# Low weight parts of the channel projection formed by ScalarE and an accumulating DMA; the second norm's token scale applied behind the down projection

## The chip, the cores and the metric

The kernel runs on one core of a Trainium2 chip. The metric is the device time of one execution in microseconds, the median over runs. The core's engines, by the names of the profile, are PE (TensorE, the matmuls), DVE (VectorE), ACT (ScalarE), POOL (GpSimd) and SP (SyncE, which issues nearly all DMAs). Each engine works through its own list of instructions in a fixed order and waits at an instruction until what it needs is there; 16 DMA engines move data beside them.

## The reference, cut to what matters

One layer of a hybrid decoder, on 512 prompt tokens and 8 x 8 sample tokens (576 in all), with a model width of 1024:

```python
x = residual
xn = rmsnorm(x, g1)
u = xn @ W_in                       # channels (q, k, v, gate) of the gated-delta mixer,
                                    # and q, k, v of the window attention
o = concat(gated_delta(conv(u)), dilated_attention(u))
h = x + o @ W_out
z = rmsnorm(h, g2)                  # h * g2 * R, one scale R for each token
y = h + (relu(z @ W_up) ** 2) @ W_down      # W_up 1024 x 4096, W_down 4096 x 1024
```

As relu(R a)^2 = R^2 relu(a)^2 for a positive R, the token scale R of the second norm can stand in front of the up projection, behind its relu, or behind the down projection as R^2.

## The kernel before, in words

**Products.** Every float32 operand of the large products is split in a high part, which the PE multiplies at full speed, and a low part that holds the rest (high = the value rounded by a copy, low = value - high). A product is then three matmuls that add up in one PSUM tile: high x high, high x low, low x high. Tokens stand along the free axis; 576 tokens are two halves of 288, so nearly every matmul is 128x128 by 128x288. A weight chunk is a raw tile `wr` (512 KB, loaded by SP); ACT copies it to `wh` (high), then another engine subtracts and writes `wl` (low). `wr` is free again after that.

**The order of the instructions.** The body of the kernel is a set of generators (tasks) that yield between steps. A recorder runs them against a model of the engines, takes at each point the task whose next step can start first (with a bias for some of them, last lines of the kernel), and so writes one fixed list for each engine. Every operation goes through a helper, so the profile's lines are those of the helpers: L262 `mm` (matmul), L265 `tr` (transpose on PE), L270 `act` (ACT), L278 `tt`, L282 `ts`, L285 `stt` (DVE: two tensors; tensor and scalar; tensor, scalar and tensor), L308 `pool_tt`, L311 `pool_cp`, L314 `pool_set`, L317 `pow_m_half` (POOL, the power -1/2), L321 `dma` (SP). Buffers come from pools with a cap for each use (`cap`), taken by `get` and given back by `rel`.

**The stages**, in microseconds of the span:
- 0 to 99: first norm, and the attention's projection (PSUM tile `pa`).
- 99 to 297: `proj_b`, the channel projection, in 16 chunks of 128 channels. A chunk is 48 matmuls into two `pg` tiles (8 blocks of 128 inputs x 3 matmuls x 2 halves; `gemm`). `wh` and `wl` have two buffers each, so chunk c+2 is split when chunk c has been multiplied. Between the chunks' matmuls the PE does the prompt's window attention (`sc` scores, DVE and ACT turn them into `e`, `ptp` transposes, `pv`), the sample attention (`s`, `pts`, `os`), whose cached keys and values are 48 loads of 512 KB (`kv`, `morekv`), and what prepares the gated delta rule. POOL writes 15 of the 16 `wl`, and small things (`cv` copies, decay `at`, a power `rk`).
- 297 to 418: the gated-delta chain, with the attention's half of the output projection (`pg<-mob,...`) as filler, and then the delta half (`pg<-moa,...`, 16 groups of 12 matmuls). `after_o` adds each result to the residual tile `h1[m]` (shown as `h`).
- 418 to 446: the way into the MLP. For each of the 16 groups `after_o` makes z = h x g2 (ACT, `xq<-h,cp`) x S (DVE, `xq<-xq,S`; S is a first scale of the token; R, made later, is what the second norm's scale still lacks). `x_parts` splits z into high and low (`xf0` to `xf3`, parts 0 to 3 of each), `t_sums` forms differences of z's blocks and splits them too (parts 4 to 7), and `square_sum` adds up the squares of h (`sq`, `acc`). At the end `stats2` sums `acc` over the partitions (`ssum`, 10 matmuls), takes the power -1/2 on POOL (`R`), and spreads it over all partitions (`rowb`, 5 transposes, then ACT to S).
- 446 to 814: the MLP. Groups u0 to u15 are the up projection, each 256 hidden channels; groups d the down projection, each after two u. u0 and u1 are classical (`up_classical`, parts 0 to 3 of xf alone), the others use seven products in place of eight (`up`, which also takes parts 4 to 7). `up_relu` and `up_out` write relu(.) x S (DVE, `stt`) to `uq`, `up_square` squares and splits it to `hid`, and `add_down` adds the down product to h1. Behind the last group each half tile of h1 goes out by a DMA (output `yT`).

The two places that the change touches most, before it:

```python
on_pool = chunk["b", 0] <= i < chunk["b", 15]                       # splitter
(pool_tt if on_pool else tt)(l[:, :cols], r[:, :cols], f(h[:, :cols]), OP.subtract)
...
act(z, x, scale=C["g2"][:, m:m + 1])                                # after_o
tt(z, z, st2["S"][:, c0:c1], OP.mult)
...
stt(Q[u].q[2 * hf + r], P, 0.0, st2["S"][:, c0:c1], OP.max, OP.mult)    # up_relu
```

Of the kernel before, what the change touches and what calls it, by code (L numbers as in the profile page):

```python
# [212 lines left out]
def hymba_step(ctx: ExitStack, tc: tile.TileContext, a):  # L213
# [30 lines left out]
    def sig(x):  # L244
        fl.do(lambda: done.add(x))
# [74 lines left out]
    def dma(dst, src, mark=None, slow=1):  # L320
        fl.op("SP", 4 * slow * size(dst) * dst.shape[0] / 360.0, lambda: nc.sync.dma_start(dst, src), mark)  # L321

    go_on = lambda t: None
# [14 lines left out]
                      "mr": 2, "ms": 2, "mw": 6})  # L338
# [19 lines left out]
    items, chunk, ready = [], {}, {}  # L358
# [141 lines left out]
    def splitter():  # L500
        for i, (src, cols) in enumerate(items[:MLP]):
# [504 lines left out]
    def gemm(wh, wl, x_h, x_l, nk, stride, off, after, extra=0):  # L1006
# [12 lines left out]
    def proj_b():  # L1019
# [4 lines left out]
        for c in range(16):  # L1024
# [3 lines left out]
            if c < 12:  # L1028
                u = yield from get("cv", ROW, "u")
                fl.spawn(conv(c, u, y), "conv")  # L1030
                yield from gemm(wh, wl, xh, xl, KT, 128, 0, lambda hf, p: conv_in(c, hf, p, u))
            else:
                fl.spawn(gate(c - 12, y), "conv")
                yield from gemm(wh, wl, xh, xl, KT, 128, 0, lambda hf, p: gate_in(c - 12, hf, p))
# [551 lines left out]
    def after_delta():  # L1586
# [4 lines left out]
        st2["acc"] = yield from get("k", [128, NT], "acc2")  # L1591
        st2["sq"] = yield from get("k", [128, 864], "sq2")
# [17 lines left out]
    def after_o(m, hf, p, last):  # L1610
# [14 lines left out]
        act(z, x, scale=C["g2"][:, m:m + 1])  # L1625
        yield 0
        tt(z, z, st2["S"][:, c0:c1], OP.mult)
# [4 lines left out]
    def square_sum(m, hf):  # L1632
# [3 lines left out]
        if m:  # L1636
            n = 2 * m + hf
            last = [("sq", m - 1, hf)] + [("sq", (n - 3) // 2, (n - 3) % 2)] * (n >= 5)
            if not all(x in done for x in last):
                yield lambda: all(x in done for x in last)  # L1640
            n = n % 3 * 288
            s = st2["sq"][:, n:n + 288]
# [8 lines left out]
    OF_X = {1: 0, 2: 1, 3: 3, 4: 7, 5: 4, 6: 5, 7: 6}  # L1651
# [3 lines left out]
    class Quad:  # L1655
        def __init__(self, tiles):
            self.t = tiles
            self.q = [blk(tiles[j // 2], j % 2) for j in range(8)]
# [4 lines left out]
    def quad(name):  # L1663
        t = []
        for j in range(4):
# [7 lines left out]
    def t_sums(x, key):  # L1673

        q = x.q
        tt(q[4], q[2], q[0], OP.subtract)
        yield 0
        tt(q[5], q[3], q[4], OP.subtract)
        yield 0
        fl.spawn(x_parts(x, key, 4, 2), "tsum")  # L1680
        tt(q[6], q[3], q[2], OP.subtract)
        yield 0
        tt(q[7], q[1], q[5], OP.subtract)
        yield 0
        fl.spawn(x_parts(x, key, 6, 2), "tsum")

    def x_parts(x, key, j, n):
        s, t = x.t[j // 2][:, j % 2 * 288:(j % 2 + n) * 288], x.out
# [10 lines left out]
    def x_factors(i):  # L1699

        x = hx[i] = yield from quad("xq")
        x.out = xf[i]
        sig(("xq", i))
        for hf in range(2):
            yield lambda: all(("z", 2 * i + j, hf) in done for j in range(2))
            fl.spawn(x_parts(x, ("x", i), 2 * hf, 2))
        yield 0
        yield from t_sums(x, ("x", i))
        yield lambda: have(("x", i), range(8))
        rel("q", "q", "q", "q")  # L1710
# [15 lines left out]
    def proj_o():  # L1726
# [17 lines left out]
        cap.update(g=8, mr=4)  # L1744
        sig("proj_o")

    def stats2():
        yield lambda: all(("sq", m, hf) in done for m in range(8) for hf in range(2))
        yield lambda: all(("z", m, hf) in done for m in range(8) for hf in range(2))
# [27 lines left out]
    def up_classical(u):  # L1777
# [3 lines left out]
        for i in range(4):  # L1781
            for hf in range(2):
                for r in range(2):
# [9 lines left out]
        for hf in range(2):  # L1793
            for r in range(2):
                fl.spawn(up_relu(u, hf, r, P[hf, r]))
        rel("mw", "mw", "mw", "mw")
# [24 lines left out]
    def up_relu(u, hf, r, P):  # L1821

        if ("Q", u) not in done:
            yield lambda: ("Q", u) in done
        yield lambda: "R2b" in done
        c0, c1 = HALF[hf]
# [214 lines left out]
```

## Time and profile before

| what | value |
|---|---|
| median of 3 runs | 816.44 us (815.4 to 816.6) |
| the profiled execution: its own time / its span | 818.95 us / 817.2 us |
| PE busy in the span | 792.2 us (97%) |
| DVE, ACT, POOL busy | 568.7 us (70%), 348.3 us (43%), 109.4 us (13%) |
| granted TensorE clock, mean | 0.993 of full speed |
| moved by DMA | 99.05 MB, mean 121 GB/s |
| chain that ended last, by engine | PE 73%, issue 9%, DVE 7%, DMA 6%, ACT 2%, SP's queue 2%, POOL 1% |

The span is what the trace covers; the execution's own time is 1.75 us longer. PE is busy nearly everywhere, so a change moves the time by what it does to the few stretches in which PE waits, or by new waits of PE.

### The profile page before, as it was taken

How to read it: one execution, taken by the hardware profiler on the slowest of the kernel's cores; microseconds unless marked ns; L12 is line 12 of the kernel's file. 1: busy time of each engine (PE TensorE's matmuls, PEld its weight loads, DVE VectorE, ACT ScalarE, POOL GpSimd, SP SyncE). 2: the span in 40 equal slices, each digit the busy share in tenths (PEclk: the TensorE clock that was granted, in tenths of full speed). 3: DMA queues.
4: the chain of work that ended last, by engine and by line, in shares of the span. 5: the costliest groups of instructions: out<-in, count | busy, mean ns of one | idle time of the engine just before them, and what ended most of it. 6: DMA issues, size and time to landing. Idle time of an engine off the chain costs nothing.

```text
span 817.2 us, 15699 instructions
## 1 busy us (share of the span) xinstructions
PE 792.2 (97%) x6323; PEld 728.1 (89%) x6323; DVE 568.7 (70%) x1250; ACT 348.3 (43%) x728; POOL 109.4 (13%) x128
## 2 busy tenths in 40 slices
PE   8989998999999999999997999999999999999998
PEld 8968877879778687778997999999999999999998
DVE  4366269888776785668798886768677676867642
ACT  5547453655242134443466543515343351534400
POOL 3443224134224000121000000000000000000000
PEclk9999999999999999999999999999999999999999
DMA  7732320106686799122221141404123130412302
GB/s 270 125 112 77 123 68 31 55 27 245 211 345 185 273 319 327 49 93 81 104 104 52 59 150 52 129 27 155 53 94 113 52 129 27 155 53 95 112 30 87
DMA packets 49864, 99.05 MB, mean 121 GB/s; under 512 B 12864, under 2 KB 26304, under 8 KB 49792
## 3 DMA queue, kind: packets, MB, share of 16 engines
q1 hardware_dynamic: 49792, 98.05, 36.6%
q8 instruction: 50, 0.82, 0.4%
q14 instruction: 22, 0.18, 0.1%
HBM read 88.15 MB, written 9.69 MB: 120 GB/s over the span
## 4 chain that ended last, share of the span: by engine, by line
PE 73%; issue 9%; DVE 7%; DMA 6%; ACT 2%; SPq 2%; POOL 1%; POOLq 0%; ACTq 0%; DVEq 0%
PE pg L262 53%; PE pa L262 7%; DVE y L285 2%; SPq L321 2%; PE cha L262 2%; DMA wr<-in_wk_dram 2%; DMA morekv<-in_cv_dram 1%; PE os L262 1%; PE ptp L265 1%; DMA morekv<-in_ck_dram 1%; PE cs L262 1%; DMA silvz<-dU 1%; PE sc L262 1%; PE s L262 1%; PE sn L262 1%
## 5 line engine op out<-in xcount | busy, mean ns | idle before, releaser
L262 PE MATMUL pg<-hid,mw 128*128 128x288 f32 x1536 | 204.7, 295 | 0.0
L262 PEld LDWEIGHTS pg<-hid,mw 128*128 128x128 f32 x1536 | 203.9, 188 | 0.0
L262 PE MATMUL pg<-xf,mw 128*128 128x288 f32 x1368 | 186.0, 297 | 4.6 <-ACT xf L270 3.8
L262 PEld LDWEIGHTS pg<-xf,mw 128*128 128x128 f32 x1368 | 183.7, 189 | 5.6 <-ACT xf L270 4.3
L278 DVE TENSOR_TENSOR h<-pg,h 128x288 f32<-128x288 f32 x160 | 72.5, 455 | 94.6 <-PE pg L262 93.8
L270 ACT ACTIVATE mw<-wr 128x512 fp32r<-128x512 f32 (+1 forms) x82 | 62.9, 791 | 70.8 <-PE pg L262 70.1
L262 PE MATMUL pg<-xh,wh 128*128 128x288 f32 x256 | 78.0, 305 | 0.0
L262 PE MATMUL pg<-xl,wh 128*128 128x288 f32 x256 | 78.0, 305 | 0.0
L262 PE MATMUL pg<-xh,wl 128*128 128x288 f32 x256 | 77.9, 304 | 0.0
L278 DVE TENSOR_TENSOR mw<-wr,mw 128x512 fp32r<-128x512 f32 (+1 forms) x82 | 72.4, 893 | 6.7 <-ACT mw L270 6.3
L270 ACT ACTIVATE mw<-ws 128x512 fp32r<-128x512 f32 x56 | 33.7, 627 | 45.3 <-PE pg L262 26.6
L262 PEld LDWEIGHTS pg<-xh,wh 128*128 128x128 f32 x256 | 48.4, 189 | 3.2 <-issue 3.0
L262 PEld LDWEIGHTS pg<-xh,wl 128*128 128x128 f32 x256 | 48.4, 189 | 2.8 <-issue 2.4
L262 PEld LDWEIGHTS pg<-xl,wh 128*128 128x128 f32 x256 | 48.5, 189 | 2.5 <-issue 1.9
L308 POOL TENSOR_TENSOR wl<-wr,wh 128x1024 fp32r<-128x1024 f32 x15 | 35.9, 2393 | 81.6 <-ACT wh L270 65.0
L262 PE MATMUL pa<-wh,xh 128*128 128x260 f32 (+1 forms) x128 | 43.1, 344 | 1.0 <-ACT wh L270 1.0
L262 PE MATMUL pa<-wh,xl 128*128 128x260 f32 (+1 forms) x128 | 43.6, 348 | 0.5 <-DVE xl L285 0.4
L262 PE MATMUL pa<-wl,xh 128*128 128x260 f32 (+1 forms) x128 | 42.7, 341 | 0.0
L270 ACT ACTIVATE wh<-wr 128x1024 fp32r<-128x1024 f32 (+1 forms) x40 | 38.6, 964 | 8.0 <-DMA wr<-in_wk_dram 5.1
L270 ACT ACTIVATE uq<-pg 128x288 f32<-128x288 f32 x42 | 17.1, 408 | 58.0 <-PE pg L262 58.0
L285 DVE SCALAR_TENSOR_TENSOR y<-u,cp,y 128x600 f32<-128x600 f32 x36 | 37.1, 1032 | 5.9 <-ACT u L270 3.3
L278 DVE TENSOR_TENSOR wl<-wr,wh 128x1024 fp32r<-128x1024 f32 (+1 forms) x25 | 28.4, 1134 | 16.0 <-ACT wh L270 15.9
(295 smaller groups left out, 1311.1 us busy)
## 6 DMA issues: line engine op xcount, KB each, us to landing
wr<-in_wu_dram SPq DMA_DIRECT2D x32, 512.0 KB, 3.3
wr<-in_wd_dram SPq DMA_DIRECT2D x32, 512.0 KB, 3.3
morekv<-in_ck_dram SPq DMA_DIRECT2D x20, 512.0 KB, 5.4
morekv<-in_cv_dram SPq DMA_DIRECT2D x20, 512.0 KB, 5.3
wr<-in_wb_dram SPq DMA_DIRECT2D x16, 512.0 KB, 4.0
wr<-in_wo_dram SPq DMA_DIRECT2D x8, 512.0 KB, 6.1
xr<-in_xT_dram SPq DMA_DIRECT2D x8, 288.0 KB, 5.6
h<-in_xT_dram SPq DMA_DIRECT2D x8, 288.0 KB, 7.2
```

Source lines behind the costliest of these rows:

```text
L262: lambda: nc.tensor.matmul(out, lhsT, rhs, start=start, stop=stop, skip_group_check=True))
L265: fl.op("PE", (97, 230), lambda: nc.tensor.transpose(out, in_, ident[:k, :k]))
L270: fl.op("ACT", cost, lambda: nc.scalar.activation(out, in_, func, bias=bias, scale=scale, accum_out=accum), mark)
L278: dve(lambda: nc.vector.tensor_tensor(out, x, y, op=op), out, x, mark=mark)
L285: dve(lambda: nc.vector.scalar_tensor_tensor(out, x, s, y, op0=op0, op1=op1), out, x, 61 if ap(s) else 0, mark=mark)
L308: fl.op("POOL", (135 + size(x) / 0.47) * slow, lambda: nc.gpsimd.tensor_tensor(out, x, y, op=op), mark)
L321: fl.op("SP", 4 * slow * size(dst) * dst.shape[0] / 360.0, lambda: nc.sync.dma_start(dst, src), mark)
```

## The change

Three parts go together.

**The channel projection's low parts.** For all 16 chunks ACT now writes `wl` = -`wh` behind `wh`, `wr` is given back, and a DMA issued by POOL reads the same weights from HBM a second time and adds them onto `wl` in SBUF (`dma_add`; it reads 512 KB from HBM, and reads and writes 512 KB of `wl`). `gemm` has a new argument `late`: for these chunks each half first does its 16 matmuls with `wh`, and then the 8 with `wl`, which wait until the DMA has landed.

**The second norm's scale.** `hid` is made without R. When `stats2` has the mean square R2 = 1/R^2, it is spread to S, all of h1 is multiplied by S (`scale_h`, 8 operations of 128x576 on DVE) before the first down product is added, and 1/R2 is spread to the tile `acc2` by five more transposes. Behind the last addition each half tile of h1 is multiplied by `acc2` (16 operations, DVE) and then goes out. POOL's power is no longer needed there. S and `acc2` stay in use through the MLP; the cap of `g` (PSUM) is 7 until they are ready and then 8.

**The way into the MLP.** z is one `stt` on DVE (h x g2 x S). `t_sums` works in place, so `xq` has two tiles in place of four, and runs only when parts 0 to 3 of all four xf are there. The sums of squares are put behind other work (bias 1500), so that they are formed while u0 to u3 run. relu is ACT's, without S (`uq<-pg` from PSUM, or `uq` in place), and `up_classical` takes its four results one after the other.

```diff
+    def dma_add(dst, src, mark):
+        fl.op("POOL", 900, lambda: nc.gpsimd.dma_start(dst, src, accum_op=OP.add), lambda t: mark(t + 7000))
...
-            on_pool = chunk["b", 0] <= i < chunk["b", 15]
-            (pool_tt if on_pool else tt)(l[:, :cols], r[:, :cols], f(h[:, :cols]), OP.subtract)
-            mark(ready, i, (h, l))
-            rel("wr")
+            if chunk["b", 0] <= i <= chunk["b", 15]:
+                act(l, f(h), scale=-1.0, mark=lambda t, i=i, v=(h, l): ready.update({i: (v, t)}))
+                rel("wr")
+                yield 0
+                dma_add(l, src, lambda t, i=i: lows.update({i: t}))
+            else:
+                tt(l[:, :cols], r[:, :cols], f(h[:, :cols]), OP.subtract)
+                mark(ready, i, (h, l))
+                rel("wr")
...
-                mm(p, wl[:, s], x_h[:, j, c0:c1], False, j == nk - 1, extra=extra)
+                if late is None:
+                    mm(p, wl[:, s], x_h[:, j, c0:c1], False, j == nk - 1, extra=extra)
                 yield 0
+            if late is not None:
+                if late not in lows:
+                    yield lambda: late in lows
+                fl.at(lows[late])
+                for j in range(nk):
+                    mm(p, wl[:, j * stride + off:j * stride + off + 128], x_h[:, j, c0:c1], False, j == nk - 1, extra=extra)
+                    yield 0
...
-        act(z, x, scale=C["g2"][:, m:m + 1])
-        yield 0
-        tt(z, z, st2["S"][:, c0:c1], OP.mult)
+        stt(z, x, C["g2"][:, m:m + 1], st2["S"][:, c0:c1], OP.mult, OP.mult)
...
-        pow_m_half(R2, R2, 5)
-        yield 0
+        yield 0
         yield from row_bcast(st2["S"], R2)
-        rel("k", "k")
+        yield 0
+        for m in range(KT):
+            fl.spawn(scale_h(m), "hsc")
+        yield lambda: all(("hs", m) in done for m in range(KT))
+        recip(R2, R2)
+        yield 0
+        yield from row_bcast(st2["acc"], R2)
+        cap["g"] = 8
         sig("R2b")
+
+    def scale_h(m):
+        tt(h1[m], h1[m], st2["S"], OP.mult)
...
-        stt(Q[u].q[2 * hf + r], P, 0.0, st2["S"][:, c0:c1], OP.max, OP.mult)
+        act(Q[u].q[2 * hf + r], P, AF.Relu)
...
         tt(h1[m][:, c0:c1], p, h1[m][:, c0:c1], OP.add)
         rel("g")
         if last:
             yield 0
+            tt(h1[m][:, c0:c1], h1[m][:, c0:c1], st2["acc"][:, c0:c1], OP.mult)
+            yield 0
             dma(a["yT"][:, m, c0:c1], h1[m][:, c0:c1])
...
-    fl.biases.update(tsum=1500, out=-30, acc=800, kv=1500, unit=30, conv=0, cs=30, levels=-50, attn=0)
+    fl.biases.update(ts=400, tsum=0, out=-30, acc=1500, hsc=1500, kv=1500, unit=30, conv=0, cs=30, levels=-50, attn=0)
```

What the recorder makes of it is seen in the lists of the engines. On the PE at the start of the channel projection (`xh`, `xl` are the parts of the normed input, `sc` attention scores) the list before reads:

```order
L262 MATMUL pa<-wl,xs_133 128x512
L262 MATMUL pg<-xh,wh 128x288
L262 MATMUL pg<-xl,wh 128x288
L262 MATMUL pg<-xh,wl 128x288
L262 MATMUL pg<-xh,wh 128x288
```

and that of the change, 16 matmuls into the same first half tile:

```order
L262 MATMUL pg<-xl,wh 128x288
L262 MATMUL sc<-qkT 128x128
L262 MATMUL sc<-mob,qkT 128x128
L262 MATMUL sc<-qkT,mob 128x128
L262 MATMUL sc<-qkT 128x128
L262 MATMUL sc<-mob,qkT 128x128
L262 MATMUL sc<-qkT,mob 128x128
L262 MATMUL pg<-xh,wl 128x288 x6
```

The first use of a chunk's `wl` has moved from the third of its matmuls to the 17th. On POOL, chunks 1 and 2 of the channel projection, before:

```order
L308 TENSOR_TENSOR wl<-wr,wh 128x1024
L311 COPY cv<-u 128x3
L311 COPY cv<-u 128x24
L314 MEMSET u 128x3
L308 TENSOR_TENSOR wl<-wr,wh 128x1024
```

and in the change:

```order
L324 DMA wl<-in_wb_dram 128x1024
L311 COPY cv<-u 128x3
L311 COPY cv<-u 128x24
L314 MEMSET u 128x3
L324 DMA wl<-in_wb_dram 128x1024
```

The DMA stands in the subtraction's place, behind the same small operations. On DVE at the end of the output projection, before, the list's piece up to the last low part that PE's first round over the four xf needs (the last row). The last addition to h1 stands 20 rows ahead of the piece; the rows between add squares, split weights and form parts of xf0, xf1 and xf2:

```order
L278 TENSOR_TENSOR xq_4975<-xq_4975,S_3880 128x288
L278 TENSOR_TENSOR xq_4976<-xq_4976,S_3880 128x288
L278 TENSOR_TENSOR xq_4975<-xq_4975,S_3880 128x288
L278 TENSOR_TENSOR xq_4976<-xq_4976,S_3880 128x288
L278 TENSOR_TENSOR xq_4977<-xq_4976,xq_4975 128x288
L278 TENSOR_TENSOR xf3_4542<-xq_4975,xf3_4542 128x576
L278 TENSOR_TENSOR xq_4977<-xq_4976,xq_4977 128x288
L278 TENSOR_TENSOR xf3_4542<-xq_4976,xf3_4542 128x576
```

and in the change, from the last addition to h1 (the first row) to that low part, with nothing left out:

```order
L278 TENSOR_TENSOR h1_4162<-pg_4833,h1_4162 128x288
L285 SCALAR_TENSOR_TENSOR xq_4567<-h1_4162,cp_74,S_4163 128x288
L278 TENSOR_TENSOR mw_4793<-wr_4778,mw_4793 128x512
L278 TENSOR_TENSOR mw_4794<-wr_4778,mw_4794 128x512
L278 TENSOR_TENSOR mw_4795<-wr_4785,mw_4795 128x512
L285 SCALAR_TENSOR_TENSOR xq_4568<-h1_4162,cp_74,S_4163 128x288
L278 TENSOR_TENSOR xf3_4557<-xq_4567,xf3_4557 128x576
L278 TENSOR_TENSOR xf3_4557<-xq_4568,xf3_4557 128x576
```

Before, 34 operations of DVE stand behind the last addition up to that low part (27 rows, some of them several operations alike); in the change 7 do, since the sums of squares and the parts 4 to 7 come later, and the parts of xf0, xf1 and xf2 stand ahead of the last addition.

## Rows read from the trace of the kernel before

**Rows 1.** Windows by stage: window, length, busy us (count) of PE PEld DVE ACT POOL, PEclk, DMA share, GB/s.

```profile
99.20:297.10 197.90, 187.89 (x1820) 157.03 (x1819) 154.37 (x450) 79.59 (x184) 54.94 (x67) 0.99 0.51 173
418.50:446.00 27.50, 22.28 (x149) 20.89 (x148) 25.74 (x57) 16.98 (x37) 1.55 (x1) 0.94 0.11 42
446.00:813.60 367.60, 367.60 (x2775) 367.55 (x2773) 250.66 (x445) 140.48 (x234) 0.00 (x0) 1.00 0.26 87
```

**Rows 2.** Windows by stage, the `pg` tiles alone: PE, PEld, DVE, ACT.

```profile
418.50:446.00 27.50, 20.82 (x134) 19.26 (x133) 1.49 (x4) 0.00 (x0) 0.94 0.11 42
```

**Rows 3.** Timeline of PE, the way into the MLP: start, us, operation, idle before.

```profile
425.81 0.40 PE L262 MATMUL pg<-xf,mw 128*128 128x288 f32 x1 [0.73 <-ACT xf L270]
433.01 0.40 PE L262 MATMUL pg<-xf,mw 128*128 128x288 f32 x1 [3.08 <-ACT xf L270]
433.80 4.31 PE L262 MATMUL pg<-xf,mw 128*128 128x288 f32 x19 [0.39 <-DVE xf L278]
437.95 1.16 PE L262 MATMUL ssum<-c,acc 128*128 128x1 f32 x10
441.24 0.65 PE L265 MATMUL rowb<-c,R 128*128 128x128 f32 x4 [0.63 <-POOL R L317]
```

**Rows 4.** Groups by form on DVE, 395 to 446 us: busy us, mean ns.

```profile
L278 DVE TENSOR_TENSOR xf<-xq,xf 128x576 fp32r<-128x576 f32 x14 | 10.3, 749 | 0.2 <-ACT xf L270 0.2
L285 DVE SCALAR_TENSOR_TENSOR uq<-pg,S 128x288 f32<-128x288 f32 x3 | 1.2, 441 | 0.0
```

**Rows 5.** Timeline, channel projection, two places: start, us, operation, idle before.

```profile
108.87 2.56 DVE L282 TENSOR_SCALAR e<-e,sm 128x256 f32<-128x256 f32 x1
108.90 2.38 POOL L308 TENSOR_TENSOR wl<-wr,wh 128x1024 fp32r<-128x1024 f32 x1 [5.34 <-issue]
111.48 0.44 PE L265 MATMUL ptp<-c,e 128*128 128x128 f32 x2 [0.43 <-DVE e L282]
137.55 2.37 POOL L308 TENSOR_TENSOR wl<-wr,wh 128x1024 fp32r<-128x1024 f32 x1
137.65 2.29 DVE L278 TENSOR_TENSOR s<-brk,rk 128x5 f32<-128x5 f32 x1
141.67 0.55 PE L265 MATMUL ptp<-c,e 128*128 128x128 f32 x3 [2.36 <-DVE e L282]
```

**Rows 6.** Waits of PE, 99 to 297 us: total, times, longest.

```profile
PE ptp L265 <- DVE e L282: 6.2, 7, 2.4
PE os L262 <- DMA morekv<-in_cv_dram: 1.8, 2, 1.1
PE s L262 <- DMA morekv<-in_ck_dram: 0.8, 1, 0.8
```

**Rows 7.** Windows by chunk, the `pg` tiles alone: PE, PEld, DVE, ACT, PEclk, DMA share.

```profile
99.20:107.97 8.77, 7.07 (x48) 6.38 (x48) 0.46 (x1) 0.00 (x0) 1.00 0.53 177
183.08:192.60 9.52, 7.25 (x50) 6.47 (x48) 0.96 (x3) 0.00 (x0) 1.00 0.59 196
192.60:200.50 7.90, 6.75 (x49) 6.42 (x49) 0.97 (x3) 0.00 (x0) 1.00 0.84 295
225.05:235.03 9.98, 6.90 (x50) 6.43 (x49) 0.95 (x3) 0.00 (x0) 1.00 1.01 403
252.00:262.10 10.10, 7.06 (x50) 6.39 (x49) 0.95 (x3) 0.00 (x0) 1.00 0.80 232
262.10:276.80 14.70, 8.17 (x51) 7.31 (x50) 0.89 (x2) 0.00 (x0) 0.88 0.83 272
```

**Rows 8.** DMA issues: count, KB each, median us to landing.

```profile
wr<-in_wb_dram SPq DMA_DIRECT2D x16, 512.0 KB, 4.0
wr<-in_wk_dram SPq DMA_DIRECT2D x4, 512.0 KB, 12.3
```

**Rows 9.** Groups by form on ACT, 99 to 297 us.

```profile
L270 ACT ACTIVATE wh<-wr 128x1024 fp32r<-128x1024 f32 x15 | 15.7, 1048 | 0.0
```

**Rows 10.** Timeline, the last operation of an engine.

```profile
813.83 0.46 DVE L278 TENSOR_TENSOR h<-pg,h 128x288 f32<-128x288 f32 x1 [1.14 <-PE pg L262]
```

More of the change, by code (lines that the diff above doesn't have):

```diff
@@ L1004, in hymba_step, with gemm @@
     UW = 604
-    def gemm(wh, wl, x_h, x_l, nk, stride, off, after, extra=0):
+    def gemm(wh, wl, x_h, x_l, nk, stride, off, after, extra=0, late=None):
         for hf, (c0, c1) in enumerate(HALF):
@@ L1637, in square_sum @@
             n = 2 * m + hf
[L1638 to L1642, printed above, removed]
+            last = ("sq", (n - 1) // 2, (n - 1) % 2)
+            if last not in done:
+                yield lambda: last in done
+            s = st2["sq"]
             act(s, x, AF.Square)
@@ L1657, in __init__, with quad @@
             self.t = tiles
-            self.q = [blk(tiles[j // 2], j % 2) for j in range(8)]
+            self.q = [blk(tiles[j // 2], j % 2) for j in range(2 * len(tiles))]
         def two(self, j):
             return self.t[j].rearrange("p (a t) -> p a t", a=2)
-    def quad(name):
+    def quad(name, n=4):
         t = []
-        for j in range(4):
+        for j in range(n):
             t.append((yield from get("q", [128, NT], name)))
@@ L1699, in x_factors @@
     def x_factors(i):
-        x = hx[i] = yield from quad("xq")
+        x = hx[i] = yield from quad("xq", 2)
         x.out = xf[i]
@@ L1705, in x_factors @@
             yield lambda: all(("z", 2 * i + j, hf) in done for j in range(2))
-            fl.spawn(x_parts(x, ("x", i), 2 * hf, 2))
-        yield 0
-        yield from t_sums(x, ("x", i))
+            fl.spawn(x_parts(x, ("x", i), 2 * hf, 2, 2 * hf))
+        yield lambda: have(("x", i), range(4)) and all(have(("x", k), range(4)) for k in range(4))
+        fl.spawn(t_sums(x, ("x", i)), "ts")
         yield lambda: have(("x", i), range(8))
-        rel("q", "q", "q", "q")
+        rel("q", "q")
     ims1 = ct([128, 5], "ims1")
@@ L1743, in proj_o @@
         rel("big", "big")
-        cap.update(g=8, mr=4)
+        cap.update(g=7, mr=4)
         sig("proj_o")
@@ L1781, in up_classical @@
         for i in range(4):
-            for hf in range(2):
-                for r in range(2):
+            for r in range(2):
+                for hf in range(2):
                     if not i:
@@ L1792, in up_classical @@
                         yield 0
[L1793 to L1796, printed above, removed]
+                    if i == 3:
+                        fl.spawn(up_relu(u, hf, r, P[hf, r]))
+                if i == 3:
+                    rel("mw", "mw")
     def factor(key, j):
@@ L1851, in up_out @@
         yield 0
-        if "R2b" not in done:
-            yield lambda: "R2b" in done
         hf, r = o // 2, o % 2
-        c0, c1 = HALF[hf]
-        stt(q[o], q[o], 0.0, st2["S"][:, c0:c1], OP.max, OP.mult)
+        if not hf:
+            act(q[o], q[o], AF.Relu)
         sig(("relu", u, hf, r))
@@ L1860, in up_square @@
     def up_square(u):
-        x = Q[u] = yield from quad("uq")
+        n = 2 if u < CLASSICAL else 3
+        x = Q[u] = yield from quad("uq", n)
         sig(("Q", u))
@@ L1866, in up_square @@
             d = x.t[hf][:, :576]
+            if hf and u >= CLASSICAL:
+                act(d, d, AF.Relu)
             act(d, d, AF.Square)
@@ L1876, in up_square @@
             yield 0
-        rel("q", "q", "q", "q")
+        rel(*["q"] * n)
     def add_down(m, hf, p, last):
         c0, c1 = HALF[hf]
+        key = "R2b" if last else ("hs", m)
+        if key not in done:
+            yield lambda: key in done
+        fl.at(rest["h", m][1])
         tt(h1[m][:, c0:c1], p, h1[m][:, c0:c1], OP.add)
@@ L1902, in mlp_gemm @@
                 continue
+            if g[1] == CLASSICAL:
+                fl.do(lambda: fl.biases.update(acc=0, hsc=0))
             if g[1] % 2 == 0:
```

40 lines of the change are left out of this document (19 added, 21 removed).

## The prediction

> **What bounds the kernel now.** I read the windows by stage first, since the share of PE over the whole span hides where it waits. In the MLP, 45% of the span, PE is busy for all of its window: 2775 matmuls in 367.60 us, a step of 0.1325 us each, and DVE and ACT have room [rows 1]. Nothing can be won there, only lost. Two stages have idle time on PE. The channel projection has 197.90 - 187.89 = 10.0 us of it. The way into the MLP has only 134 `pg` matmuls in 27.50 us [rows 2]; at the MLP's step they would take 134 x 0.1325 = 17.75 us, so 9.75 us are lost there. The change touches both, so I looked for what ends last in each.
>
> In the way into the MLP the timeline of PE shows the waits [rows 3]: 0.73 us, then 3.08 and 0.39 us for xf, made by ACT and DVE. DVE is busy for 25.74 of the 27.50 us there [rows 1], so it is DVE's queue that PE waits for: squares, products with S and parts 4 to 7 stand ahead of the xf3 that PE wants. Behind the long idle time, 19 matmuls take 4.31 us in place of 19 x 0.1325 = 2.52; the granted clock of this stage is 0.94 of the upper level, with the lower one (half) granted in a piece of it. Then `ssum` and `rowb` take PE's time themselves and add a wait of 0.63 us for POOL's power [rows 3].
>
> In the channel projection the waits of PE name one pair above all: the transposes `ptp` waiting for DVE's `e`, 6.2 us in 7 waits [rows 6]. The timeline shows what is behind it [rows 5]. A scaling of 128x256 on DVE takes 2.56 us, begun with POOL's `wl` of 2.38 us, and ends with it. At the second place an operation on 128x5, which has next to nothing to do, takes 2.29 us, and ends when POOL's 2.37 us end (137.55 + 2.37 = 139.92; 137.65 + 2.29 = 139.94). So DVE is held while POOL subtracts, and `ptp` is late by 0.43 and 2.36 us. Six of the seven waits begin in the shadow of a `wl` of POOL; the seventh, 0.28 us, does not. That leaves 5.9 us.
>
> The Trainium skill says the same of this pair (SBUF — State Buffer, Who interferes with whom): a DVE instruction with two SBUF inputs contends with a GpSimd instruction that reads SBUF. The trace agrees at the second place, two inputs and 2.29 us; at the first, 2.56 us, the second operand is a scalar for each partition.
>
> **The change, part by part.**
>
> *Way into the MLP.* Removed ahead of the last xf3: the squares, parts 4 to 7, and the separate product with S. The lists in the section on the change have 34 operations of DVE from the last addition to that low part before, and 7 after. By the rows of DVE the seven are two `stt` (0.44 each, the nearest row being `uq<-pg,S`), three weight splits of 128x512 and two low parts at 0.749 [rows 4]; the splits lie below the 0.749 of a 128x576. With ACT's two high parts, taken as long as DVE's, the path is at most 2 x 0.44 + 7 x 0.749 = 6.1 us. It is covered: PE has the three other xf first in u0, 3 x 24 matmuls x 0.1325 = 9.5 us. So the waits for xf and the piece at half clock should go. Of the 9.75 us, what `ssum` and `rowb` take moves into u3 and is not won: 10 `ssum` matmuls from 437.95 to 439.03 (1.1 us) and 5 transposes at about a step each, 0.66. The 0.63 of the power goes, as POOL's power is gone. I put the gain at 9.75 - 1.7 = 8.05. Bounds: 4.2 (only the three xf waits, 0.73 + 3.08 + 0.39) and 9.75. The second set of `rowb` adds 0.66.
>
> *DVE held by POOL.* The 15 subtractions go. A DMA's issue on POOL takes their place. ACT gets 16 operations more of 1.05 us [rows 9], in a stage where it is busy for 79.59 of 197.90 us. The attention chain is not shorter otherwise, so some waits may reappear behind ACT's `e`: a 1.05 us copy in its way. Bounds: 0 (each wait comes back in another form) and 5.9. I take 5.0, near the rows.
>
> *The accumulating DMA.* No row shows one. It moves 512 KB from HBM as a `wr` load does, and reads `wl` in SBUF besides. Landing bounds: 4.0 us, a plain `wb` load of the same bytes, and 12.3 us, a `wk` load in the crowded first stage [rows 8]. I take 8.0, twice the plain load, for twice the bytes read. The room it has: buffers of chunk c+1 come free when chunk c-1 ends, so the time is chunk c's length, plus the first 16 matmuls of c+1 (2.1 us), minus two ACT operations (2.1), minus about 1.4 us for semaphores and the issue on POOL (an estimate: two hand-overs of about a quarter of a microsecond each, as PE's 0.39 in rows 3 bounds one, and 0.9 for the issue). So room = length - 1.4. The lengths are those of rows 7: six of the fifteen are short, 8.77, 9.52, 7.90, 9.98, 10.10 and (the chunk from 276.8 to 286.9) 10.10 again, with rooms of 7.4, 8.1, 6.5, 8.6, 8.7 and 8.7. The other nine are 12.2 us or longer (rooms of 10.8 and more). At a landing of 8 us, PE waits 0.6 + 1.5 = 2.1 us; at 4.0, nothing; at 10, 2.6 + 1.9 + 3.5 + 1.4 + 1.3 + 1.3 = 12.0; at 12.3, about 30. That is the steepest term. Short chunks are also those with the most other DMA work (a share of 0.84 and 1.01) [rows 7], which speaks for late landings just there. Value +2.1, bounds 0 and +30.
>
> The Trainium skill's fit for a DMA issued by GpSimd is 2.0 us + bytes / 436e3 (DMA: Bandwidth & Descriptors, Anatomy of one DMA — SWDGE (gpsimd) path): 3.2 us for 512 KB, an estimate of 4.4 with the bytes doubled. No run here shows one yet; the plain load by SP has 4.0. By it PE would wait nowhere, and the sum would be 2.1 us lower.
>
> *Waits for cached keys and values* (1.8 + 0.8 us [rows 6]) and the half-clock piece between 262 and 277 us (0.88 over 14.70 us, so 14.70 x 0.12 = 1.8 us [rows 7]): 8.4 MB more go through the same DMA engines, SP's weight loads come earlier, and the sample attention stands later in PE's list. Signs differ; I take 0.
>
> *MLP.* u3 and the first d now hold `ssum`, two sets of `rowb` and 8 products of 128x576 (0.749 each at most, 6.0 us of DVE) ahead of the first down addition, with a PSUM cap of 7. DVE has 367.6 - 250.7 = 117 us idle in the MLP, less the squares that moved in. I take +0.5, bounds 0 and 3.
>
> *Tail.* One more DVE operation lies between the last addition and the output DMA: 0.46 by the last row [rows 10], say +0.4.
>
> **Sum:** -8.05 + 0.66 - 5.0 + 2.1 + 0 + 0.5 + 0.4 = -9.4 us. The profiled execution took 818.95 us, so 809.6 for such a one; it lies 2.5 us over the median of the runs shown, so the median should be 816.44 - 9.4 = **807 us**.
>
> **Rivals.**
>
> *The adds land late and decide (slower).* Place: the first `wl` matmul of each chunk, 17th in its list. The other terms give 11.5 us, so the change loses from a landing of about 9.9 us on; at 12.3 it is 816.4 - 11.5 + 30 = 835. For it: nothing in the trace shows that such a DMA is as quick as a load, and it reads what it writes. Against: a load of the same size needs 4.0 us, 12.3 is seen only in the first stage, and POOL has little else to do.
>
> *The adds land late without deciding,* at 9 to 10 us: 6 to 12 us of waits, 811 to 817. A mechanism for it: if DVE's operations hold POOL while it prepares the transfer, as POOL's hold DVE now, each issue waits for one more operation; at about 0.75 us [rows 4] the landing goes from 8.0 to 8.75, and the waits from 2.1 to 4.6 us, so 809.5. The Trainium skill has such a rule (SBUF — State Buffer, SBUF: two separate sides): while DVE runs an operation in a 2-port mode, GpSimd cannot write its DMA's descriptors. No run here shows it yet.
>
> *Larger gain.* Landing as quick as a load (2.1 us less), the 2.6 us for keys and values and the 1.8 us of clock go, and the DVE term is whole (0.9): 816.4 - 9.4 - 7.4 = 799.6.
>
> *No relief on DVE.* POOL's issue or ACT's second copy delays `e` as the subtraction did: the 5.0 us stay, 812. The stall of the way into the MLP may also come back in u3, at a price of up to 3 us: 815 with both.
>
> **How the numbers follow.** The forecast (802 to 812, with both smaller mishaps at its upper end) 0.60; larger gain, below 802, 0.11; late without deciding, 812 to 817, 0.14; late and decisive, above 817, 0.13; no change for a reason that I don't see 0.02. What a measurement of this kernel can tell from no change is about 0.2%, 1.6 us. Of the third case, 0.08 lies below 814.8, 0.05 within and 0.01 above. So faster 0.60 + 0.11 + 0.08 = 0.79, same 0.05 + 0.02 = 0.07, slower 0.14. The range that leaves 2 in 10 out runs from 799 (the larger gain worked out) to 816 (the late case without its end).
>
> **What the profile after would show.** DVE's operations on 128x5 back at a fraction of a microsecond, and `ptp` waits of PE below 1 us in all. No wait for xf over 0.5 us between 418 and 430, and no half clock there; u0 without gaps. `wl` issues landing in 8 us, with PE waits for `wl` only in the chunks that follow a short one. `ssum` in u3 without a wait on either side. If the prediction is wrong, I expect it at the waits of PE for `wl`, in several microseconds for each chunk; next at the waits for `e` unchanged under another releaser.

## The result, and the profile after

The changed kernel takes 826.7 us (median of 4 runs, 821.85 to 828.24) beside 816.52 us for the kernel before: a ratio of 1.0100, 95% interval 1.0063 to 1.0136. It is slower by 10 us, where 9 us faster were forecast. The profiled execution took 827.54 us, with a span of 825.7 us and a mean granted clock of 0.986 (0.993 before). Ratios, here and below, leave out slow executions, those that took over 1.5% longer than the fastest of their kernel.

I split the span by the first and last `pg` product of each kind:

| stage | before | after | difference | forecast |
|---|---|---|---|---|
| to the first product of the channel projection | 99.2 | 97.2 | -2.0 | 0 |
| from there to the first product of the MLP | 319.3 | 334.8 | +15.5 | -2.9 |
| from there to the last product of the MLP | 395.0 | 389.5 | -5.5 | -6.9 |
| tail | 3.7 | 4.2 | +0.5 | +0.4 |

So the way into the MLP gave nearly what was forecast, and the middle, channel projection to output projection, gave back three times as much. (The first row is a fall of the clock at 44.9 us that this execution does not have; the profile of e6 below, with the lists of the changed kernel, has one at 45.0 us.)

**What went as forecast.** The timeline of PE at the way into the MLP; before, three waits stood here [rows 3]:

```profile
431.99 15.22 PE L262 MATMUL pg<-xf,mw 128*128 128x288 f32 x113
...
463.19 6.62 PE L262 MATMUL pg<-xf,mw 128*128 128x288 f32 x48 [0.40 <-DVE mw L278]
470.27 9.88 PE L262 MATMUL pg<-xf,mw 128*128 128x288 f32 x70 [0.47 <-DVE mw L278]
```

113 matmuls without a gap up to the end of that view at 447 us, no wait for xf and no half clock. Two small waits for weights split on DVE are new, where the squares now run. In the tail the new product with `acc2` stands behind the last addition [rows 10]:

```profile
821.82 0.46 DVE L278 TENSOR_TENSOR h<-pg,h 128x288 f32<-128x288 f32 x1 [0.64 <-PE pg L262]
822.32 0.46 DVE L278 TENSOR_TENSOR h<-h,acc 128x288 f32<-128x288 f32 x1
```

DVE is no longer held by POOL. The groups by form on DVE, 97 to 432 us, before (mean ns is the last number ahead of the idle time):

```profile
L282 DVE TENSOR_SCALAR e<-e,sm 128x256 f32<-128x256 f32 x8 | 5.0, 622 | 0.1
...
L278 DVE TENSOR_TENSOR s<-brk,rk 128x5 f32<-128x5 f32 x4 | 4.9, 1236 | 0.1
```

and after:

```profile
L282 DVE TENSOR_SCALAR e<-e,sm 128x256 f32<-128x256 f32 x8 | 2.8, 350 | 0.1
...
L278 DVE TENSOR_TENSOR s<-brk,rk 128x5 f32<-128x5 f32 x4 | 1.9, 478 | 0.1
```

**What did not.** The waits of PE from 97 to 440 us, against [rows 6]:

```profile
PE ocT L265 <- DVE smp L292: 3.6, 1, 3.6
PE s L262 <- DMA morekv<-in_ck_dram: 2.9, 1, 2.9
PE os L262 <- DMA morekv<-in_cv_dram: 1.8, 2, 1.2
...
PE ptp L265 <- DVE e L282: 0.5, 1, 0.5
```

The 6.2 us for `ptp` have shrunk to 0.5, and no wait for `wl` is left to see. But PE waits longer for cached keys, and 3.6 us for a transpose of the sample attention (`ocT`) behind DVE, whose queue stands at a small DMA (`smp`, 8 KB). Waits in all are much what they were, as these two take up what `ptp` gave back, so they don't explain 15 us. The granted clock does for the larger part; windows of 20 us (PEclk is the third number from the end):

```profile
220.00:240.00 20.00, 17.13 (x147) 12.40 (x144) 8.32 (x24) 8.00 (x11) 1.19 (x3) 0.83 0.86 307
260.00:280.00 20.00, 16.74 (x173) 13.54 (x174) 14.11 (x67) 4.65 (x8) 1.83 (x2) 0.91 0.88 286
300.00:320.00 20.00, 20.00 (x241) 16.72 (x241) 10.72 (x31) 8.12 (x29) 1.92 (x1) 0.95 0.87 298
320.00:340.00 20.00, 20.00 (x176) 15.15 (x176) 7.81 (x23) 5.13 (x21) 0.00 (x0) 0.71 0.34 119
```

(1 - 0.83 + 1 - 0.91 + 1 - 0.95 + 1 - 0.71) x 20 = 12.0 us lost to the lower level, against 1.8 before in this stage. The first two falls come with the wait for cached keys and the one for the transpose. In the timeline and in the chain that ended last it is seen which transfers were late (in the chain the second number is the time from issue to landing):

```profile
211.73 0.92 POOL L324 DMA_DIRECT2D wl<-in_wb_dram  x1 [1.51 <-ACT wl L270]
...
223.06 1.08 PE L262 MATMUL s<-morekv,qbd 128*32 128x256 f32 x8 [2.87 <-DMA morekv<-in_ck_dram]
...
255.06 0.88 POOL L324 DMA_DIRECT2D wl<-in_wb_dram  x1 [6.80 <-ACT wl L270]
```

```profile
213.22 9.81 DMA morekv<-in_ck_dram
...
255.28 6.46 DMA smp<-sl
```

Both were issued by SP right behind a sum of POOL, the keys 1.5 us after it and `smp` 0.2 us.

The last and longest fall follows no wait. There PE has only the small products of the delta chain and of the late sample attention. The `pg` products alone, after and before, in the stretch between the channel projection's last `wh` products and the first of the output projection:

```profile
286.00:367.80 81.80, 1.48 (x12) 1.26 (x11) 0.46 (x1) 0.00 (x0) 0.92 0.63 225
```

```profile
296.70:332.00 35.30, 0.54 (x4) 0.31 (x3) 0.44 (x1) 0.00 (x0) 1.00 0.79 265
```

The stretch without large products has grown from 35 to 82 us: the output projection's attention half may start only when the sample attention is done, and its last product with cached values came at 360.5 us in place of 323.4.

The DMA part of the page after (queue 0 is POOL's; share of the 16 engines at the end), against [rows 8]:

```profile
q1 hardware_dynamic: 49792, 98.05, 35.6%
q0 software_dynamic: 2304, 8.39, 6.0%
...
morekv<-in_ck_dram SPq DMA_DIRECT2D x20, 512.0 KB, 7.3
...
wl<-in_wb_dram POOLq DMA_DIRECT2D x16, 512.0 KB, 6.4
```

The sums land in 6.4 us, inside every room. But 6.0% of 825.7 us over 16 of them are 3.1 us of all 16 DMA engines for each, where 98.05 MB in 35.6% make about 1.6 us for a plain load of that size. The cached keys take 7.3 us to land (median) in place of 5.4. The median alone is no measure of the loss: it is 7.4 us in the run with plain copies below, which loses next to nothing by them; what counts are the two transfers above, for which PE waits.

### The profile page after: what moved, and what is told of

Read it like the earlier page. It is cut to its first block, busy times and chain, and to the rows that moved or that the text cites. A ratio compares the mean times of both kernels' runs of the same rounds, so it can differ in the third digit from the quotient of the medians.

```text
span 825.7 us, 15766 instructions
## 1 busy us (share of the span) xinstructions
PE 804.2 (97%) x6328; PEld 734.4 (89%) x6328; DVE 537.8 (65%) x1210; ACT 378.3 (46%) x780; POOL 85.9 (10%) x128
## 3 DMA queue, kind: packets, MB, share of 16 engines
q1 hardware_dynamic: 49792, 98.05, 35.6%
q0 software_dynamic: 2304, 8.39, 6.0%
## 4 chain that ended last, share of the span: by engine, by line
PE 82%; DVE 6%; DMA 5%; ACT 4%; issue 1%; SPq 1%; POOL 1%; ACTq 0%; DVEq 0%; POOLq 0%
PE pg L262 57%; PE pa L262 7%; PE cha L262 2%; PE os L262 2%; PE sc L262 2%; DMA wr<-in_wk_dram 1%; PE s L262 1%; PE ptp L265 1%; SPq L321 1%; PE pv L262 1%; DMA morekv<-in_ck_dram 1%; PE sn L262 1%; PE cs L262 1%; PE pu L262 1%; PE py L262 1%
## 5 line engine op out<-in xcount | busy, mean ns | idle before, releaser
L262 PE MATMUL pg<-xf,mw 128*128 128x288 f32 x1368 | 184.0, 295 | 0.9 <-DVE mw L278 0.9
L278 DVE TENSOR_TENSOR h<-pg,h 128x288 f32<-128x288 f32 x160 | 72.5, 456 | 99.2 <-PE pg L262 99.2
L262 PE MATMUL pg<-xh,wh 128*128 128x288 f32 x256 | 73.0, 306 | 0.5 <-DVE E L285 0.5
L262 PE MATMUL pg<-xl,wh 128*128 128x288 f32 x256 | 72.7, 306 | 0.0
L270 ACT ACTIVATE uq<-pg 128x288 f32<-128x288 f32 x64 | 25.8, 403 | 76.2 <-PE pg L262 76.1
L262 PE MATMUL pg<-xh,wl 128*128 128x288 f32 x256 | 43.5, 303 | 0.0
L278 DVE TENSOR_TENSOR mw<-ws,mw 128x512 fp32r<-128x512 f32 x56 | 37.6, 684 | 5.4 <-ACT mw L270 5.3
L278 DVE TENSOR_TENSOR hid<-uq,hid 128x576 fp32r<-128x576 f32 x32 | 24.1, 753 | 23.6 <-ACT hid L270 23.6
L262 PEld LDWEIGHTS pg<-xh,wl 128*128 128x128 f32 x256 | 36.6, 190 | 2.8 <-issue 2.3
L278 DVE TENSOR_TENSOR wl<-wr,wh 128x1024 fp32r<-128x1024 f32 (+1 forms) x24 | 27.1, 1131 | 15.5 <-ACT wh L270 15.4
```

The source lines that it names most:

```text
L262: lambda: nc.tensor.matmul(out, lhsT, rhs, start=start, stop=stop, skip_group_check=True))
L270: fl.op("ACT", cost, lambda: nc.scalar.activation(out, in_, func, bias=bias, scale=scale, accum_out=accum), mark)
L278: dve(lambda: nc.vector.tensor_tensor(out, x, y, op=op), out, x, mark=mark)
```

## The experiments

Spans scatter with the clock, so each run is read by two numbers: its time, and span x mean granted clock, an estimate of what the span would be at the upper level throughout. It holds where PE is what bounds: in ten runs of the changed kernel the clock lay between 0.977 and 0.996 and the span between 817.1 and 833.8 us, while the product stayed within 813.0 to 817.7. It holds nearly as well in the stretch without large products, where it could fail because PE has only small products there. From the channel projection's last product to the first of the output projection, e11 and e9 (below) have lists of nearly the same length, e11 at the upper level and e9 in part at the lower:

```profile
291.20:329.10 37.90, 35.92 (x417) 27.98 (x414) 25.69 (x63) 18.86 (x77) 5.24 (x3) 1.00 0.68 235
```

```profile
295.70:349.10 53.40, 50.16 (x414) 39.04 (x412) 25.10 (x64) 19.78 (x81) 0.00 (x0) 0.74 0.49 166
```

53.40 x 0.74 = 39.5 us, against 37.90. Medians of all runs, and the ratio to the kernel before on the same chip with its interval:

| kernel | time, us | ratio | clock | span x clock, us |
|---|---|---|---|---|
| before (31 runs) | 818.4 | 1 | 0.993 | 810.8 |
| the change again (e5) | 827.4 | 1.0090 (1.0057 to 1.0123) | 0.988 | 815.3 |
| second and third part alone (e1) | 812.4 | 0.9894 (0.9819 to 0.9969) | 0.996 | 807.2 |
| the same again (e12) | 813.1 | 0.9924 (0.9898 to 0.9949) | 0.996 | 808.1 |
| first part alone (e2) | 832.4 | 1.0164 (1.0092 to 1.0236) | 0.986 | 819.4 |
| sums of 16 columns (e3) | 815.1 | 0.9967 (0.9930 to 1.0005) | 0.998 | 810.4 |
| sample attention early (e4) | 825.9 | 1.0000 (0.9959 to 1.0041) | 0.986 | 811.7 |
| full sums in chunks 0 to 7 only (e6) | 820.0 | 1.0019 (0.9996 to 1.0042) | 0.990 | 810.4 |
| full sums in chunks 8 to 15 only (e7) | 828.4 | 1.0120 (1.0087 to 1.0152) | 0.987 | 816.4 |
| plain copies (e8) | 820.5 | 0.9995 (0.9958 to 1.0032) | 0.990 | 810.7 |
| 16 columns and early (e9) | 826.1 | 1.0080 (1.0060 to 1.0101) | 0.976 | 805.0 |
| sums in chunks 0 to 3, POOL from 4 on (e10) | 808.7 | 0.9872 (0.9857 to 0.9888) | 0.998 | 805.3 |
| sums in 0 to 7, POOL from 8 on, early (e11) | 812.1 | 0.9919 (0.9881 to 0.9957) | 0.990 | 802.4 |
| e9 with doubled products (e13) | 825.5 | 1.0088 (1.0065 to 1.0111) | 0.996 | 820.3 |
| the change with doubled products (e14) | 845.8 | 1.0345 (1.0308 to 1.0382) | 0.997 | 842.4 |

**Which part.** e1 takes the first part back, e2 puts it alone into the kernel before; the core of e1, and e2 is its reverse:

```diff
-            if chunk["b", 0] <= i <= chunk["b", 15]:
-                act(l, f(h), scale=-1.0, mark=lambda t, i=i, v=(h, l): ready.update({i: (v, t)}))
...
+            on_pool = chunk["b", 0] <= i < chunk["b", 15]
+            (pool_tt if on_pool else tt)(l[:, :cols], r[:, :cols], f(h[:, :cols]), OP.subtract)
```

> The change without its first part: the low parts of the channel projection are POOL's subtractions again, and PE's list of the channel projection and the delta chain is the one of the kernel before. The theory of order says that all of the loss came with the first part, through the order that it gave to the sample attention: the way into the MLP gave back 5.5 us net in the changed kernel, so about 811 us here. If the loss lay in the MLP or in the new norm, this would stay above 816 us.

> The first part alone, put into the kernel before: ACT's negative copy, the accumulating DMA, the 16 low matmuls last. The stage from the channel projection to the end of the output projection took 15.5 us longer in the changed kernel and the stage ahead of it 2 us less. The theories of order and of traffic both say about 830 us (816.5 + 13.5), with the half clock near 222 us and near 318 us again. If the parts only hurt together, about 817 us.

Both came near what was expected (812.4 and 832.4 us): the second and third part win 6 us, and the first loses 14 us by itself (3 and 9 us at equal clock). It is the first part that is to be explained.

**Order or traffic.** The first theory was that of the order: the recorder put the sample attention later. e3 leaves all lists alone and cuts the traffic; e4 keeps the traffic and changes the order.

```diff
-                dma_add(l, src, lambda t, i=i: lows.update({i: t}))
+                dma_add(l[:, :16], src[:, :16], lambda t, i=i: lows.update({i: t}))
```

> The changed kernel with the same lists on all engines, but each accumulating DMA adds only 16 of the 1024 columns of the low part (the other low parts are left as the negative upper part, so the output differs): the 8.4 MB of traffic are gone. Theory of order: the same time as the changed kernel, 824 to 828 us, with the last sample attention product still near 360 us. Theory of traffic (the sums read memory while the cached keys are loaded, 7.3 us to landing in place of 5.4): 812 to 816 us, and the 2.9 us wait for the cached keys near 220 us gone.

```diff
-        fl.op("POOL", 900, lambda: nc.gpsimd.dma_start(dst, src, accum_op=OP.add), lambda t: mark(t + 7000))
+        fl.op("POOL", 900, lambda: nc.gpsimd.dma_start(dst, src, accum_op=OP.add), lambda t: mark(t + 10000))
```

> The changed kernel with one number of the recorder's model changed, from 7000 to 10000 for the landing of the accumulating DMA, which makes it put the sample attention early again: its first product behind 392 matmuls of the channel projection (483 in the changed kernel, 407 before), and 168 of its 224 value products ahead of the projection's end (88, and 168 before). The traffic is the same as in the changed kernel. Theory of order: the attention half of the output projection starts near 332 us again and the time is 806 to 812 us. Theory of traffic: still 822 us or more.

e3 fell on the side of traffic, 815.1 us, against the theory of order. In its waits, 97 to 440 us, the cached keys are no longer late:

```profile
PE os L262 <- DMA morekv<-in_cv_dram: 1.4, 3, 0.6
...
PE s L262 <- DMA morekv<-in_ck_dram: 0.3, 1, 0.3
```

The two transfers of the section above, at the same places of SP's list (the keys issued at 213.56 us, `smp` at 250.3), land in 5.9 us in place of 9.8 and in 3.4 in place of 6.5, and the wait of `ocT` is 1.0 us in place of 3.6:

```profile
morekv<-in_ck_dram SPq DMA_DIRECT2D x1, 512.0 KB, 5.9
...
smp<-sl SPq DMA_DIRECT2D x1, 8.0 KB, 3.4
```

The two waits together are 5.2 us longer in the change than in e3, and 6.0 us longer in e7 (below), whose excess over e3 at equal clock is 6.0.

e4 met neither expectation: five of its ten runs lie at 818.7 to 820.5 us with clocks of 0.992 to 0.994, five at 831 to 835 us with 0.971 to 0.981. At equal clock it is 3.6 us better than the change. The new number moves more than the sample attention (the first chunk of the projection, with what stands between its products, takes 16.6 us in place of 11.9), so it prices the whole order.

**Which of the sums.** Same lists again, with 16 columns in one half of the chunks.

```diff
-                dma_add(l, src, lambda t, i=i: lows.update({i: t}))
+                w = cols if i < chunk["b", 8] else 16
+                dma_add(l[:, :w], src[:, :w], lambda t, i=i: lows.update({i: t}))
```

(e6; e7 has the condition the other way round, e5 no edit.)

> The changed kernel once more, beside the three that follow: 822 to 828 us, the stage from the start of the channel projection to the end of the output projection some 335 us long.

> The changed kernel with the same lists; chunks 0 to 7 keep the full accumulating DMA, which land before 195 us, and chunks 8 to 15 add only 16 of 1024 columns (the rest of those low parts is left as the negative upper part, so the output differs). The theory that the sums cost time only where the cached keys and values are loaded too (185 to 325 us) says as with all sums cut, 812 to 816 us. The rival, that the sums hurt the projection itself wherever they stand (late landings, ACT or DVE held), says half of the excess here, about 820 us.

> The counterpart: chunks 0 to 7 add 16 columns, chunks 8 to 15 are full (the output differs as before). The theory of the cached keys says the whole excess, 822 to 828 us, with half clock between 215 and 340 us; the rival says about 820 us.

At equal clock the sums of chunks 0 to 7 cost nothing (810.4, as e3) and those of 8 to 15 cost 6.0 us (816.4), which is all of it. In plain time e7 has the whole excess, as the theory of the cached keys says. e6, at 820.0 us, has the number of the rival, but its clock is lower than that of e3 (0.990 against 0.998): its run at 0.997 took 815.0 us, and that of e3 at 0.997 took 815.2. In the profile of e6 the waits for keys and for `ocT` are 0.4 us each, so the sums of the early chunks do not hurt where they stand.

**What of the transfer.**

```diff
-        fl.op("POOL", 900, lambda: nc.gpsimd.dma_start(dst, src, accum_op=OP.add), lambda t: mark(t + 7000))
+        fl.op("POOL", 900, lambda: nc.gpsimd.dma_start(dst, src), lambda t: mark(t + 7000))
```

> The changed kernel with the same lists; the DMA of POOL copies the weights onto the low part in place of adding them (the output differs). By the queues' shares of the changed kernel an accumulating DMA of 512 KB takes 16 engines x 3.1 us (6.0% of 825.7 us for 16 of them) and a plain one about 1.6 us (35.6% for 98.05 MB). If it is the time of the DMA engines that counts, about half of the excess goes: some 818 to 821 us. If it is the number of bytes fetched from memory, or the queue of POOL, that counts, it stays at 822 to 828 us.

820.5 us lies in the range forecast for the time of the DMA engines, but that is the clock's doing: at equal clock nothing is left beside e3 where half of the excess was expected, and the three runs at a clock of 0.999 took 812.8 to 813.8 us, as e3's do. The landings do follow the engines' time: 7.2 us for that load of keys (5.9 in e3, 9.8 in the change) and 4.6 for `smp` (3.4 and 6.5). PE waits 1.1 us for keys and 1.7 for `ocT`. That is 1.5 us more than in e3, with half of the engines' time of the sums, against 5.2 more in the change: the loss is not in proportion to the engines' time. The queue's row, to be held against the 6.0% above:

```profile
q0 software_dynamic: 2304, 8.39, 3.3%
```

3.3% of 811.0 us over 16 copies are 1.7 us of the engines for each; the accumulating ones take 3.1. The Trainium skill (Collectives: The Full Stack, The bandwidth ceiling: the fold count and why AG ≠ RS ≠ AR) says of the sum in a ReduceScatter between cores that it needs two source reads, and comes out at half the rate of a copy. The trace agrees with the rate here, with a factor of 1.8, for a sum of HBM and SBUF; the second read is not seen in it (2304 packets in either case).

**Does the order cost time too?**

> Both suspects taken away: each sum adds only 16 of 1024 columns (the output differs), and the recorder's 10000 puts the sample attention early again, as in the run before with that number. The runs so far give 815.1 us without the traffic in the order of the changed kernel, and 812.4 us with the second and third part alone. If the order that the first part gave to the sample attention costs time by itself, and hides the relief on DVE, 806 to 810 us here. If order costs nothing and the relief on DVE is worth nothing, 813 to 816 us.

The time missed both expectations, 826.1 us; at equal clock it is 805.0, 5.4 us under e3, the relief that was looked for. The clock takes more than that back, so the relief is an estimate: no run of e9 kept its clock. In the profiles the order of e3 has the shorter projection (180 us against 195) and loses it again behind: its stretch without large products holds 829 matmuls in 76 us, that of e9 the 414 above. Windows of e9:

```profile
300.00:320.00 20.00, 17.22 (x213) 14.30 (x212) 10.76 (x27) 11.41 (x48) 0.00 (x0) 0.99 0.91 294
320.00:340.00 20.00, 20.00 (x114) 14.93 (x113) 6.13 (x15) 3.56 (x13) 0.00 (x0) 0.50 0.20 74
340.00:360.00 20.00, 20.00 (x150) 14.42 (x148) 9.88 (x35) 8.51 (x35) 5.00 (x3) 0.83 0.03 8
```

PE runs at the lower level from 319.7 us for 27 us, most of it with little traffic.

**Sums in the early chunks alone.** In e10 (diff) and e11 (8 in place of 4, and the 10000 of e4), POOL subtracts in the later chunks as before, and `late` holds only for the chunks with a sum.

```diff
-            if chunk["b", 0] <= i <= chunk["b", 15]:
+            if chunk["b", 0] <= i < chunk["b", 0] + 4:
```

> A kernel that computes all of it: accumulating DMAs for chunks 0 to 3 alone, POOL's subtraction from chunk 4 on, the second and third part as in the change. The sample attention has the order of the kernel before (first product behind 407 matmuls, 168 of 224 value products ahead of the projection's end), and the sums land before the cached keys are loaded. The waits of PE behind DVE in chunks 1 to 3 (0.43 + 1.38 + 0.49 + 2.36 us before) should go: 812.4 - 4.7 = 808 us, 807 to 811. If the sums hurt wherever they stand: 812 us or more.

> A kernel that computes all of it: accumulating DMAs for chunks 0 to 7, POOL's subtraction from chunk 8 on, and the recorder's 10000 for the landing, with which the sample attention comes early (first product behind 385 matmuls). All six waits behind POOL's subtraction lie in chunks 1 to 6, so up to 5.9 us go: 812.4 - 5.9 = 806.5 us, 805 to 811, if the order costs nothing more. Over 812 us, if the sums of chunks 6 and 7, or the early sample attention, cost what the relief brings.

> The second and third part alone once more, beside the two versions: 811 to 814 us.

e10 came as forecast, 808.7 us with all four runs within 0.2 us, faster than the kernel before by 1.3% and than e12 by 4.4 us. At equal clock it is 2.8 us under e12 and 1.9 under e1, so a part of the 4.4 is the clock. Its waits for `ptp`, and those of e12:

```profile
PE ptp L265 <- DVE e L282: 1.6, 3, 0.8
```

```profile
PE ptp L265 <- DVE e L282: 6.2, 7, 2.4
```

e11 reached 807.4 us in its best run and 802.4 us at equal clock, lower than all others, some 5.3 us beside e1 and e12 (807.2 and 808.1); this is the relief together with another order. Its clock varies, and so its times, up to 830.3; the median, 812.1, lies just over the range expected.

**What brings the lower clock.** A product that starts a PSUM group gives the same result when issued twice; e13 and e14 do so between the end of the channel projection and the end of the sample attention.

```diff
-              lambda: nc.tensor.matmul(out, lhsT, rhs, start=start, stop=stop, skip_group_check=True))
+              lambda: [nc.tensor.matmul(out, lhsT, rhs, start=start, stop=stop, skip_group_check=True)
+                       for _ in range(2 if start and fl.more else 1)])
```

> The kernel with small sums and the early sample attention (826.1 us; granted clock 0.976, with 27 us at half clock from 319.7 us on), with one thing added: between the end of the channel projection and the end of the sample attention, each product that starts a PSUM group is issued twice, which leaves the result as it is. 89 small matmuls more, no other list changed. If PE at half clock is a consequence of too little work on PE while the filler of the output projection is missing, the clock stays up and the time falls below 820 us in spite of the added work. If the clock falls for another reason, the clock stays at 0.976 and the time is 826 to 834 us.

> The changed kernel (827 us, clock 0.986 to 0.988 in most runs) with the same doubling: 147 small matmuls more in the same stretch. If sparse work on PE is what brings the half clock there, the clock rises to 0.993 or more (what is left are the falls near 222 and 262 us, behind waits of PE) and the time is 818 to 824 us. If not, 827 us and more at the same clock.

The clock did what the theory said: 0.976 to 0.996, and 0.988 to 0.997. The window of e13 in the stretch that ran at half clock in e9:

```profile
320.00:350.00 30.00, 30.00 (x298) 25.16 (x297) 12.19 (x40) 9.19 (x33) 3.08 (x2) 1.00 0.07 24
```

More work on PE in this stretch kept the clock up in all eight runs. The times did not fall: 825.5 and 845.8 us. I had taken PE to have room for the added products in this stretch. At equal clock 89 of them (each is two matmuls in the trace) cost 820.3 - 805.0 = 15.3 us and 147 cost 27.1, some 0.18 us each: they lie on the path, and eat up or exceed what the clock gives back.

## Why the prediction was wrong

- **Way into the MLP** (-8.05 + 0.66 + 0.5): right in mechanism, measured -5.5 us in place of -6.9 for the MLP with its way in. Two new waits of 0.9 us for split weights are in the difference, within the bound of 3 us.
- **DVE held by POOL** (-5.0): right in mechanism. `ptp` waits fell from 6.2 to 0.5 us. What that is worth by itself is less sure: 1.9 to 2.8 us at equal clock for the first four chunks (e10, where 4.7 were expected), and some 5.3 with eight chunks and another order (e11). The Trainium skill's rule on the two engines (SBUF — State Buffer, Who interferes with whom) holds by its counterpart too: without POOL's subtraction the operation on 128x5 falls from 1236 to 478 ns.
- **The accumulating DMA** (+2.1): looked for in the wrong place. The sums landed in 6.4 us, sooner than the 8.0 taken, and PE never waited for `wl`, so the term was 0. The feared rival, sums that land late and decide, did not come, nor did a hold of POOL by DVE show: POOL's issues took 0.9 us each. The Trainium skill's rule on descriptors (SBUF — State Buffer, SBUF: two separate sides) is neither shown nor refuted by that, since no landing was waited for. The Trainium skill's fit (DMA: Bandwidth & Descriptors, Anatomy of one DMA — SWDGE (gpsimd) path) gave an estimate of 4.4 us; the measured 6.4 lies between it and my 8.0.
- **The step that failed** is the one that I set to nothing: "8.4 MB more go through the same DMA engines, SP's weight loads come earlier, and the sample attention stands later in PE's list. Signs differ; I take 0." Both halves cost. The engines' time for the sums of chunks 8 to 15, 8 x 3.1 us, falls into the stretch in which 48 loads of keys and values keep them 0.8 busy: 6.0 us at equal clock (e7 against e3), through the late load of keys and the late `smp`. The order with the later sample attention costs 3.6 to 5.4 us at equal clock (e4 against e5, e9 against e3), and so eats the relief on DVE: the stretch in which the delta chain and the sample attention run without the filler grew from 35 to 82 us.
- **The clock** was priced only where a wait was seen to precede its fall. In the three profiles with full sums in the late chunks and the order of the change (the change, e5, e7) it falls at the waits for keys and for `ocT`, and in those of e3, e6 and e8, where these waits are short, it does not. The long fall in the stretch without filler is in the profiles of the change and of e6, and not in those of e3, e5, e7 and e8, which have the same lists. 0.988 against 0.993 over 825 us are 4 us, about half of the 10 us; the other half is the 4.5 us between 815.3 and 810.8.

Sum at equal clock, from the runs: 810.8 - 3.2 (second and third part) - 5.3 (DVE) + 5.4 (order) + 4.9 (traffic, e5 against e3) = 812.6, where 815.3 was measured; 2.7 us stay open, as much as e9 lies over e11 (805.0 against 802.4), which has POOL's subtraction in chunks 8 to 15. Open too is why the same program keeps its clock in one execution and loses it in the next (e4, e11), and why e9 loses it in all four runs while e10, with the order of the kernel before, does not. The length of the stretch without large products does not tell: it is 35 us in e10 and 55 in e9, where 27 us at the lower level make it longer, but the 77 us of e3 kept the clock in its profile.

## What to carry to other kernels

A transfer that nobody waits for still takes its engines' time from others: before a compute step is turned into a DMA, look at what else is loaded in that stretch, and put a price on the delay of those loads. Here the same replacement pays in the first four chunks, ahead of the cached keys (808.7 us), and costs 6.0 us at equal clock in the last eight, where two transfers that PE waits for stand right behind a sum. When a recorder or scheduler re-orders a whole stage after a local change, compare when the large filler products can start; that moved by 36 us here, and the new order cost about as much (3.6 to 5.4 us at equal clock) as the waits that the change removed.

## What was not expected of the hardware

An accumulating DMA of 512 KB took 1.8 times the engines' time of a plain copy (3.1 against 1.7 us) and landed in 6.4 us against 4.4 for the copy. The granted clock can fall with PE nowhere idle for long: in the changed kernel it fell at 318.1 us, within 20.00 us in which PE counted as busy throughout. In e9, where the longest wait in the 12 us ahead was 1.2 us, it stayed at its lower level for 27 us while PE counted as busy for all of 20.00 us in a window, with 114 small matmuls in it, and it stayed up when 89 products more were put into this stretch (e13).
